# Second tiles of a pair turned through three PSUM banks, and w_down differences tied in order to products

## The chip, the cores and the metric

The kernel runs on one core of one Trainium2 chip. The metric is device time in microseconds (us) of one execution, as a median of three runs. A profile is one further execution, taken by the hardware profiler. PE is TensorE (matmuls and transposes), DVE is VectorE, ACT is ScalarE, POOL is GpSimd, SP is SyncE, whose queue issues most of the transfers.

## The reference

One decoder layer in float32 with S = 2048 tokens and D = 1024 channels. The feed-forward part, in which the change lies, has D_FF = 2816:

```python
hn = rms_norm(h, mix_pre_g)
proj = hn @ w_in                      # q, k, v and the convolution's input
attn_out = sliding_window_attention(q, k, v, attn_sinks, rel_bias)
conv_out = conformer_conv(u, ...)     # GLU, causal depthwise conv width 31, LayerNorm, swish, pointwise
mixed = jnp.concatenate([attn_out, conv_out], axis=-1) @ w_out
h = h + rms_norm(mixed, mix_post_g)
hn = rms_norm(h, ffn_pre_g)
ff = (jax.nn.silu(hn @ w_gate) * (hn @ w_up)) @ w_down
h = h + rms_norm(ff, ffn_post_g)
```

## The kernel before, in words

**Tiles and stages.** The tokens are cut into four tiles of 512 (tile 0 to 3). A tile passes through stages named by a letter that every buffer's name carries behind the @: A (input projection), B (attention), C (convolution taps, which DVE multiplies and adds into `fc` buffers), W (output projection, residual, norms), H (the normed tile turned so that channels lie on partitions, and operands made of it), F (gate and up products) and G (products with w_down, and the output). The work of several stages is emitted interleaved, by costs written beside each `yield`; a tile scheduler then fixes the order of each engine's instructions before the run. On the chip each engine works through its own order strictly and waits where a semaphore is not yet up.

**Products.** A float32 product is made of three matmuls on rounded parts: for each operand ACT copies the high part (`split_f`, L821) and DVE subtracts it from the operand to get the low part (`lo`, L825, recorded at L94 like nearly every DVE operation). A product of stage F is 12 matmuls of 128x512 into one of four `mm` banks of PSUM (L85). There are three banks called `tr` and one called `ct`; `tr` is used by the attention and by part of W, `ct` by the turns of H.

**Pairs of tiles.** Tiles 0 and 1, and tiles 2 and 3, are multiplied together with w_gate and w_up by a Strassen-Winograd scheme: seven products of half-size blocks in place of eight. Its token operands are called B11 and B21 (of the first tile of a pair), B22 (of the second) and T1 to T4 (sums over both). While the second tile is in stage W, stage F already runs the products that need the first tile only (`stage_pre`): a first half with B11, whose results go to DRAM (`keeps`), and a second half with B21, which is *seeded*: SP loads a kept result into a `gb` buffer (L923), ACT copies it into the PSUM bank (L939), and the 12 matmuls add to it. After that `stage_p1` runs the remaining products, which need T1 to T4 and B22.

**The turns and the sums.** At the end of stage W, `norm_w` holds the normed tile in four `chl` buffers. For the second tile of a pair (w = 1 and 3) it calls `turn_row` eight times. Each call takes a bank, does four 128x128 transposes on PE (L816), and has ACT copy the bank into a `mid` buffer, scaled by g_ffn (L817). The `chl` buffers come free with the last turn. `stage_h_sums` then makes the operands of the pair in four blocks of 256 channels: SP loads the first tile's turned rows from DRAM (`hT`, L868) into a `chl` buffer, DVE forms the sums (`chl@H`), and each sum is split by ACT and DVE into a high and a low part (`hl@H`, `ql@H`, `mid@H`, `p@H`, `yt@H`, `mb@H`).

**The differences of w_down.** The products with w_down use a like scheme, and its weight differences are made once, in `stage_tsums`, which runs beside the products of stage F of the first pair. For each of 11 pairs of row blocks POOL issues four loads of w_down (L1106) into a `wx` buffer (a ring of one) and two `fc` buffers (a ring of three, shared with the convolution taps), DVE subtracts four times (L1111, recorded at L94, `wx@G` and `fc@G`), and POOL issues four stores to DRAM (`td`, L1112).

**Ties.** `mat` (L77) records every matmul of a product in `made["rows"]`. The DVE wrapper (L86) already gives the convolution taps an order-only dependency on such a matmul: the scheduler has to place the tap behind it, but nothing waits on the chip.

Of the kernel before, what the change touches and what calls it, by code (L numbers as in the profile page):

```python
# [18 lines left out]
ALU = mybir.AluOpType  # L19
# [18 lines left out]
def layer_kernel(ctx, tc, x, xT, cols, rows, sinks, relb, onehot, w_in, w_pw, w_out, w_gate, w_up, w_down, out):  # L38
# [19 lines left out]
    def f4(tag, shape=(P, D)):  # L58
        return t_(tag, shape)

    def f2(tag, shape=(P, T)):
        return t_(tag, shape)
# [8 lines left out]
    def bank(tag, bufs):  # L71
        return ps.tile([P, T], F32, tag=tag, name=nm(tag), bufs=bufs)

    mm = lambda: bank("mm", 4)
    tr = lambda: bank("tr", 3)
    ct = lambda: bank("ct", 1)
# [4 lines left out]
    pace = {"main": None, "tied": None}  # L81
    made = {"rows": [], "at": 0, "new": True}
# [9 lines left out]
    def dve(op):  # L92
        def emit(*args, **kw):
            r = op(*args, **kw)  # L94
            if not paced[0]:
                pace["main"] = r.ins
            elif pace["main"] is not None and pace["main"] is not pace["tied"]:
                tc.add_manual_dep(
                    r.ins,
                    pace["main"].name,  # L100
                    mybir.DependencyInfo(mybir.DependencyClass.NoSync, mybir.DependencyReason.DATA),
                    reason="conv taps keep pace with the projections",
                )
                pace["tied"] = pace["main"]
            if paced[0] and made["rows"]:
                made["new"] = True
                tc.add_manual_dep(
                    r.ins,
                    made["rows"][min(made["at"], len(made["rows"]) - 1)].name,
                    mybir.DependencyInfo(mybir.DependencyClass.NoSync, mybir.DependencyReason.DATA),  # L110
                    reason="conv taps keep pace with the products",
                )
                made["at"] += TIE
            return r

        return emit

    stt = dve(nc.vector.scalar_tensor_tensor)
    vtt = dve(nc.vector.tensor_tensor)
# [639 lines left out]
    def norm_w(w, acc):  # L759
# [35 lines left out]
        if w == 0:  # L795
            normed.extend(xs)
        elif w == 2:
            for k in range(KC):
                u = turn_row(w, xs, k, f2("gb"))
                nc.scalar.dma_start(hT[1][k], u)  # L800
                yield 2.0
        else:
            for k in range(4):
                t = t_("mid", (P, 2, T))
                for j in range(2):
                    turn_row(w, xs, k + 4 * j, t[:, j])
                    yield 2.0
                normed.append(t)
# [2 lines left out]

    def turn_row(w, xs, k, u):
        lab[0] = f"H{w}"
        b = ct()
        for s in range(4):
            nc.tensor.transpose(b[:, s * P : (s + 1) * P], xs[s][:, k * P : (k + 1) * P], ident)  # L816
        act(u, b, AF.Copy, scale=g_ffn[:, k : k + 1])  # L817
        return u
# [27 lines left out]
    def stage_h_plain(ws, ops, n, off):  # L846
        L = f"H{ws[0]}"
        for k in range(4):
            lab[0] = L
            if ws[0]:  # L850
                u = f2(COLTAG[ws[0]][k])
                nc.sync.dma_start(u, hT[ws[0] // 2][k + off])
            else:
                u = turn_row(0, normed, k + off, f2("gb"))
                lab[0] = L
                nc.scalar.dma_start(hT[0][k + off], u)
            o = op_tile(ws, ops, n, k, {})
            act(o[:, 0], u, AF.Copy)
            lo(u, o, False)
            yield 2.0  # L860
# [238 lines left out]
    def stage_tsums(td):  # L1099
        L = "G0"  # L1100
        for pr in range(NF // 2):
            lab[0] = L
            wx = f4("wx", (P, 2, T))
            b = [wx[:, 0], wx[:, 1], f2("fc"), f2("fc")]
            for i, (f, n) in enumerate(((0, 0), (0, 1), (1, 0), (1, 1))):
                nc.gpsimd.dma_start(b[i], w_down[2 * pr + f, :, n * T : (n + 1) * T])  # L1106
            yield 3.9
            b11, b12, b21, b22 = b
            for to, o, p_, q_ in ((0, b11, b12, b11), (2, b12, b22, b12), (1, b22, b22, b11), (3, b21, b21, b22)):
                lab[0] = L  # L1110
                vtt(o, p_, q_, ALU.subtract)  # L1111
                nc.gpsimd.dma_start(td[to, pr], o)  # L1112
                yield 0.25

# [326 lines left out]
    lh.add("S0", stage_h_sums(ws, ops), lambda: "N1" in lh.done)  # L1441
    run(stage_pre(ws, ops, mids[0], keeps[0], Q0))
    lt.add("TS", stage_tsums(td))
    run(stage_p1(ws, ops, mids[0], keeps[0]))
    lt.until("TS")
# [80 lines left out]
```

## Time and profile before

| what | value |
|---|---|
| time, median of 3 runs | 1982.09 us (1979.29 to 1984.77) |
| the profiled execution | 1987.9 us, of which its span is 1986.2 us |
| PE busy | 1930.4 us, 97% of the span |
| PEld (weight loads, beside PE) | 1546.7 us, 78% |
| DVE busy | 1476.3 us, 74% |
| ACT busy | 961.8 us, 48% |
| POOL busy | 304.3 us, 15% |
| granted TensorE clock, mean | 0.987 of full speed |
| transfers | 435.67 MB, mean 219 GB/s |

The span is the time from the first to the last recorded instruction; 1.7 us of the profiled execution lie outside it. Busy shares are means over the whole span. The rows of a window show, for each engine, its busy us and the count of its instructions, then the granted clock as a share of full speed, the mean busy share of the 16 DMA engines, and what they moved in GB/s. Rows of a timeline show start, duration, engine, line, operation, output and inputs; what stands in square brackets is the idle time of the engine before it and what ended it.

### The profile page before, as it was taken

What the parts mean: (1) busy time and instruction counts of PE and PEld (TensorE: products, weight loads), DVE (VectorE), ACT (ScalarE), POOL (GpSimd) and SP (SyncE); (2) the same over time, 40 slices, a digit from 0 to 9 for tenths busy, and PEclk for the clock granted to TensorE, in tenths of its full rate; (3) what the DMA queues carried; (4) which work ended last, traced back from release to release, by engine and by line L of the source; (5) the groups of instructions that cost most, each with busy time, mean ns of one, the idle gap of its engine ahead of it and who ended that gap; (6) DMA issues with size and microseconds to landing.
All of it is one profiled execution on the core that took longest, in us unless ns stands there. A gap on an engine that the chain in (4) does not pass through costs nothing.

```text
span 1986.2 us, 26652 instructions
## 1 busy us (share of the span) xinstructions
PE 1930.4 (97%) x8730; PEld 1546.7 (78%) x8730; DVE 1476.3 (74%) x2648; ACT 961.8 (48%) x1886; POOL 304.3 (15%) x427
## 2 busy tenths in 40 slices
PE   8999999999999699999999999999899999999997
PEld 6877777777777588778888878887688888888886
DVE  5999969995874899787759965666866775555557
ACT  5455354447647544334345464656533433345443
POOL 4011011111121101220000110000023332311003
PEclk9999999999999799999999999999899999999999
DMA  8787657566658668775478777759844542375664
GB/s 311 251 303 219 210 187 256 185 212 214 225 195 281 232 218 266 260 266 184 130 253 276 259 255 242 249 202 309 293 140 169 179 140 96 132 244 181 211 195 144
DMA packets 209578, 435.67 MB, mean 219 GB/s; under 512 B 21752, under 2 KB 39328, under 8 KB 209440
## 3 DMA queue, kind: packets, MB, share of 16 engines
q1 hardware_dynamic: 191648, 402.52, 60.7%
q0 software_dynamic: 7040, 23.07, 3.5%
q10 hardware_dynamic: 10752, 8.39, 1.3%
q8 instruction: 68, 1.11, 0.2%
q14 instruction: 70, 0.57, 0.1%
HBM read 323.26 MB, written 110.63 MB: 218 GB/s over the span
## 4 chain that ended last, share of the span: by engine, by line
PE 77%; DVE 8%; DMA 7%; issue 3%; POOL 2%; ACT 2%; SPq 0%; DVEq 0%; POOLq 0%; ACTq 0%
PE mm@F L85 32%; PE mm@G L85 16%; PE mm@A L85 15%; PE mm@W L85 4%; PE tr@B L85 4%; PE tr@W L85 2%; DVE fc@C L94 2%; DMA wx@G<-w_down 1%; DMA gb@F<-keeps 1%; PE mm@U L85 1%; DVE w@F L94 1%; DVE hl@G L94 1%; PE tr@B L491 1%; DMA td<-wx@G 1%; DMA fc@G<-w_down 1%
## 5 line engine op out<-in xcount | busy, mean ns | idle before, releaser
L94 DVE SCALAR_TENSOR_TENSOR fc@C<-glu@C,colt,fc@C 128x512 f32<-128x512 f32 x480 | 357.3, 758 | 2.6
L85 PE MATMUL mm@F<-hl@H,w@F 128*128 128x512 f32 x1056 | 261.3, 397 | 10.2 <-ACT mm@F L939 10.2
L85 PEld LDWEIGHTS mm@F<-hl@H,w@F 128*128 128x128 f32 x1056 | 201.0, 192 | 54.6 <-ACT mm@F L939 12.5
L85 PE MATMUL mm@G<-hl@G,hl@G 128*128 128x512 f32 x924 | 227.7, 393 | 1.1 <-DVE hl@G L94 1.1
L821 ACT ACTIVATE w@F<-chl@F 128x512 fp32r<-128x512 f32 x220 | 135.9, 626 | 187.8 <-PE mm@F L85 149.6
L85 PE MATMUL mm@A<-hl@A,w@A 128*128 128x512 f32 x840 | 209.5, 397 | 4.2 <-ACT w@A L127 1.5
L85 PEld LDWEIGHTS mm@G<-hl@G,hl@G 128*128 128x128 f32 x924 | 171.7, 188 | 37.3 <-DVE hl@G L94 1.9
L85 PE MATMUL mm@G<-w@G,hl@G 128*128 128x512 f32 x876 | 199.4, 389 | 0.0
L85 PEld LDWEIGHTS mm@G<-w@G,hl@G 128*128 128x128 f32 x876 | 164.4, 188 | 34.1
L85 PEld LDWEIGHTS mm@A<-hl@A,w@A 128*128 128x128 f32 x840 | 156.6, 189 | 42.9 <-issue 3.3
L94 DVE TENSOR_TENSOR w@F<-chl@F,w@F 128x512 fp32r<-128x512 f32 x198 | 151.4, 768 | 49.0 <-ACT w@F L821 48.8
L85 PE MATMUL mm@F<-mid@H,w@F 128*128 128x512 f32 x528 | 136.5, 398 | 20.3 <-ACT w@F L821 13.3
L85 PEld LDWEIGHTS mm@F<-mid@H,w@F 128*128 128x128 f32 x528 | 101.0, 192 | 43.7 <-ACT w@F L821 14.1
L85 PE MATMUL mm@F<-ql@H,w@F 128*128 128x512 f32 x528 | 130.0, 392 | 0.0
L85 PE MATMUL mm@F<-p@H,w@F 128*128 128x512 f32 x528 | 129.1, 389 | 0.0
L85 PE MATMUL mm@F<-x@H,w@F 128*128 128x512 f32 x528 | 126.9, 391 | 0.0
L85 PEld LDWEIGHTS mm@F<-ql@H,w@F 128*128 128x128 f32 x528 | 99.1, 189 | 20.8
L85 PEld LDWEIGHTS mm@F<-p@H,w@F 128*128 128x128 f32 x528 | 99.1, 188 | 20.6
L85 PEld LDWEIGHTS mm@F<-x@H,w@F 128*128 128x128 f32 x528 | 98.4, 188 | 21.1 <-issue 0.8
L127 ACT ACTIVATE w@A<-raw@A 128x512 fp32r<-128x512 f32 x110 | 67.5, 626 | 92.1 <-PE mm@A L85 62.1
L94 DVE TENSOR_TENSOR w@G<-raw@G,w@G 128x512 fp32r<-128x512 f32 x73 | 52.1, 713 | 73.0 <-ACT w@G L821 71.8
L494 POOL TENSOR_SCALAR_AFFINE_SELECT p@B<-p@B 128x512 f32<-128x512 f32 x62 | 51.7, 843 | 338.4 <-ACT p@B L492 337.1
(314 smaller groups left out, 3290.1 us busy)
## 6 DMA issues: line engine op xcount, KB each, us to landing
mids<-fa@F SPq DMA_DIRECT2D x154, 256.0 KB, 2.7
raw@A<-w_in SPq DMA_DIRECT2D x55, 512.0 KB, 4.6
w@A<-lo_in SPq DMA_DIRECT2D x84, 256.0 KB, 3.3
fc@G<-mids SPq DMA_DIRECT2D x77, 256.0 KB, 3.4
fa@G<-mids SPq DMA_DIRECT2D x75, 256.0 KB, 4.4
gb@F<-keeps SPq DMA_DIRECT2D x72, 256.0 KB, 3.5
w@W<-fold SPq DMA_DIRECT2D x32, 512.0 KB, 5.9
raw@F<-w_gate SPq DMA_DIRECT2D x22, 512.0 KB, 4.0
```

The lines of the kernel that those rows point to most:

```text
L85: r = nc.tensor.matmul(*args, **kw)
L94: r = op(*args, **kw)
L127: act(w[:, 0], raw, AF.Copy)
L491: nc.tensor.transpose(o[:, i * P : (i + 1) * P], pr[:, 4 * g + i], ident)
L494: nc.gpsimd.affine_select(out=pg[:, kb].rearrange("p (i q) -> p i q", q=P), in_=pg[:, 1].rearrange("p (i q) -> p i q", q=P), compare_op=AL ...
L821: act(w[:, 0], x, AF.Copy)
```

## The change

`turn_row` takes its bank from the ring of three `tr` banks where w is odd, so for tiles 1 and 3; tiles 0 and 2 keep the one `ct` bank. In `stage_tsums` each of the 44 subtractions gets an order-only dependency on the product matmul that was emitted last. No instruction is added or taken away.

```diff
     def turn_row(w, xs, k, u):
         lab[0] = f"H{w}"
-        b = ct()
+        b = tr() if w % 2 else ct()
         for s in range(4):
             nc.tensor.transpose(b[:, s * P : (s + 1) * P], xs[s][:, k * P : (k + 1) * P], ident)
...
                 lab[0] = L
-                vtt(o, p_, q_, ALU.subtract)
+                r = vtt(o, p_, q_, ALU.subtract)
+                tc.add_manual_dep(
+                    r.ins,
+                    made["rows"][-1].name,
+                    mybir.DependencyInfo(mybir.DependencyClass.NoSync, mybir.DependencyReason.DATA),
+                    reason="weight differences keep pace with the products",
+                )
                 nc.gpsimd.dma_start(td[to, pr], o)
```

The change moves instructions, since the scheduler orders them anew. Each name below carries the number of its buffer, which is the same in both programs.

PE, before, among the seeded products of the first pair: one turn of tile 1, between matmuls of one product (`mm@F_1010`; `chl@W_938` to `941` are the four normed row blocks).

```order
L85 MATMUL mm@F_1010_6103<-hl@H_802_4927,w@F_994_6037 128x512 x3
L85 MATMUL mm@F_1010_6103<-hl@H_810_4970,w@F_994_6037 128x512 x3
L85 MATMUL mm@F_1010_6103<-hl@H_813_4981,w@F_994_6037 128x512 x3
L816 MATMUL ct@H_972_5927<-ident,chl@W_938_5731 128x128
L816 MATMUL ct@H_972_5927<-ident,chl@W_939_5733 128x128
L816 MATMUL ct@H_972_5927<-ident,chl@W_940_5735 128x128
L816 MATMUL ct@H_972_5927<-ident,chl@W_941_5737 128x128
L85 MATMUL mm@F_1010_6103<-hl@H_821_5028,w@F_994_6037 128x512 x3
```

PE, after, at the last product with B11 and the first seeded one (`mm@F_997`, `mm@F_996`): three turns begin together.

```order
L85 MATMUL mm@F_997_6044<-x@H_787_4853,w@F_975_5940 128x512 x3
L816 MATMUL tr@H_968_5902<-ident,chl@W_938_5731 128x128
L816 MATMUL tr@H_972_5927<-ident,chl@W_938_5731 128x128
L816 MATMUL tr@H_974_5934<-ident,chl@W_938_5731 128x128
L85 MATMUL mm@F_997_6044<-x@H_799_4916,w@F_975_5940 128x512 x3
L85 MATMUL mm@F_996_6042<-hl@H_802_4927,w@F_982_5975 128x512 x3
L85 MATMUL mm@F_996_6042<-hl@H_810_4970,w@F_982_5975 128x512
L816 MATMUL tr@H_968_5902<-ident,chl@W_939_5733 128x128
L816 MATMUL tr@H_968_5902<-ident,chl@W_940_5735 128x128
L816 MATMUL tr@H_972_5927<-ident,chl@W_939_5733 128x128
L816 MATMUL tr@H_974_5934<-ident,chl@W_939_5733 128x128
```

The eight turns of tile 1 stood one to every second product, with the last in product F_1081. They now stand in groups of three, three and two, with the last in F_1022, ten products earlier.

DVE, before, just ahead of `w@F_1104`, the first weight split that `stage_p1` needs for T1. The last split of a seeded product, `w@F_1092`, stands 52 rows ahead of it.

```order
L94 TENSOR_TENSOR chl@H_1059_6351<-chl@H_1059_6351,chl@H_1066_6379 128x512
L94 TENSOR_TENSOR wx@G_1119_6658<-fc@G_1121_6660,wx@G_1119_6658 128x512
L94 TENSOR_TENSOR ql@H_1071_6409<-chl@H_1066_6379,ql@H_1071_6409 128x512
L94 SCALAR_TENSOR_TENSOR fc@C_1083_6465<-glu@C_1082_6463,colt,fc@C_1083_6465 128x512
L94 TENSOR_TENSOR p@H_1077_6436<-chl@H_1059_6351,p@H_1077_6436 128x512
L94 TENSOR_TENSOR chl@F_1103_6599<-raw@F_1100_6592,chl@F_1101_6594 128x512
L94 TENSOR_TENSOR chl@F_1102_6596<-chl@F_1102_6596,raw@F_1100_6592 128x512
L94 TENSOR_TENSOR w@F_1104_6602<-chl@F_1102_6596,w@F_1104_6602 128x512
```

DVE, after, at the same split:

```order
L94 TENSOR_TENSOR p@H_1077_6436<-chl@H_1059_6351,p@H_1077_6436 128x512
L94 TENSOR_TENSOR w@F_1089_6494<-raw@F_1085_6471,w@F_1089_6494 128x512
L94 TENSOR_TENSOR fa@F_1076_6434<-fa@F_1076_6434,mm@F_1075_6420 128x512
L94 TENSOR_SCALAR fc@C_1083_6465<-glu@C_1082_6463,colt 128x512
L94 TENSOR_TENSOR w@F_1092_6517<-raw@F_1085_6471,w@F_1092_6517 128x512
L94 TENSOR_TENSOR mid@H_1078_6439<-chl@H_1059_6351,mid@H_1078_6439 128x512
L94 TENSOR_TENSOR chl@F_1102_6596<-chl@F_1102_6596,raw@F_1100_6592 128x512
L94 TENSOR_TENSOR chl@F_1103_6599<-raw@F_1100_6592,chl@F_1101_6594 128x512
L94 TENSOR_TENSOR w@F_1104_6602<-chl@F_1102_6596,w@F_1104_6602 128x512
```

The sums of stage H and their splits now stand among the weight splits of the seeded products, and four rows lie between `w@F_1092` and `w@F_1104`. The first difference of w_down (`wx@G_1116`) moved from row 751, among the rows of stages A to C, to row 1093; pairs of differences stood some 18 rows apart and now stand some 27 apart (15 to 46).

SP, after, in the seeded half of the first pair: the loads of `hT` for the sums (`chl@H`) among the loads of kept results (`gb@F`) and of weights (`raw@F`).

```order
L923 DMA gb@F_1039_6247<-keeps_4718 128x512
L868 DMA chl@H_1019_6152<-hT_115 128x2x512
L971 DMA mids_4715<-fa@F_1017_6147 128x512
L916 DMA raw@F_1049_6300<-w_gate 128x512
L923 DMA gb@F_1043_6268<-keeps_4718 128x512
L916 DMA raw@F_1049_6300<-w_up 128x512
L868 DMA chl@H_1036_6239<-hT_115 128x2x512
L923 DMA gb@F_1050_6303<-keeps_4718 128x512
L971 DMA mids_4715<-fa@F_1029_6205 128x512
L868 DMA chl@H_1059_6351<-hT_115 128x2x512
```

Before, these three loads stood 25 rows later, at rows 410, 414 and 418 for now 385, 390 and 393, and were the neighbours of `gb@F_1093` to `gb@F_1142`. In the second pair the four loads moved from rows 865 to 881 up to rows 832 to 866, and four loads of `chl@G` from `h_scr` now stand ahead of them, at rows 823 to 826.

## The prediction

> **What bounds the kernel now.** I read the page first: what is busy, and where the clock drops.
>
> ```profile
> span 1986.2 us, 26652 instructions
> PE 1930.4 (97%) x8730; PEld 1546.7 (78%) x8730; DVE 1476.3 (74%) x2648; ACT 961.8 (48%) x1886; POOL 304.3 (15%) x427
> PEclk9999999999999799999999999999899999999999
> ```
>
> PE sets the time; a gain can come only from the 56 us in which it is not busy and from slow clock. Two slices are below 9 inside the run (slices of 49.7 us: the 14th starts at 646 us, the 29th at 1390 us). PE's waits over the whole run, as total, times and longest:
>
> ```profile
> PE mm@F L85 <- ACT w@F L821: 13.3, 2, 12.6
> PE mm@F L85 <- ACT mm@F L939: 10.2, 6, 3.3
> PE mm@F L85 <- DVE w@F L94: 5.8, 2, 3.0
> PE mm@F L85 <- DVE at@F L94: 4.8, 2, 3.3
> ```
>
> All four are in stage F: the start of `stage_p1` (w@F), the seeds (L939), and DVE's accumulation (at@F). The windows of the first place, against a stretch without a wait (DVE is the third pair of numbers; then clock, DMA share, GB/s):
>
> ```profile
> 620.00:650.00 30.00, 30.00 (x143) 24.83 (x142) 12.90 (x20) 20.04 (x37) 0.00 (x0) 1.00 0.76 244
> 680.00:690.00 10.00, 1.91 (x4) 1.09 (x5) 10.00 (x18) 4.11 (x7) 0.89 (x2) 0.50 0.54 196
> 690.00:700.00 10.00, 10.00 (x35) 7.99 (x34) 10.00 (x17) 4.01 (x7) 2.72 (x6) 0.75 0.84 286
> 650.00:700.00 50.00, 34.39 (x140) 27.34 (x140) 46.12 (x76) 25.16 (x43) 7.56 (x15) 0.80 0.72 244
> 750.00:800.00 50.00, 50.00 (x222) 41.42 (x221) 45.32 (x74) 19.60 (x35) 10.23 (x19) 1.00 0.80 272
> ```
>
> Undisturbed, PE does 222 matmuls in 50 us, 0.2252 us each. In 650 to 700 it does 140: 82 are missing, 82 x 0.2252 = 18.5 us. DVE is 12.90 us busy in the 30 of 620 to 650 and full in 680 to 700. PE's timeline shows the turns of tile 1, then the stall:
>
> ```profile
> 645.05 0.60 PE L816 MATMUL ct@H<-ident,chl@W 128*128 128x128 f32 x4
> ...
> 656.44 0.60 PE L816 MATMUL ct@H<-ident,chl@W 128*128 128x128 f32 x4
> 656.80 15.69 PE L85 MATMUL mm@F<-hl@H,w@F 128*128 128x512 f32 x68
> 685.10 1.22 PE L85 MATMUL mm@F<-mid@H,w@F 128*128 128x512 f32 x2 [12.61 <-ACT w@F L821]
> 689.31 2.08 PE L85 MATMUL mm@F<-mid@H,w@F 128*128 128x512 f32 x4 [3.00 <-DVE w@F L94]
> ```
>
> The wait names ACT, but the split it waited for is fed by DVE. DVE's timeline over the stall, from the first sum of stage H to the split that released PE, with differences of w_down in between:
>
> ```profile
> 657.39 0.68 DVE L94 TENSOR_TENSOR chl@H<-mid@W,chl@H 128x512 f32<-128x512 f32 x1
> ...
> 665.40 0.69 DVE L94 TENSOR_TENSOR wx@G<-fc@G,wx@G 128x512 f32<-128x512 f32 x1
> ...
> 688.57 0.69 DVE L94 TENSOR_TENSOR w@F<-chl@F,w@F 128x512 fp32r<-128x512 f32 x1
> ```
>
> The sums begin 1 us after the last turn; then DVE is 31.2 us without a gap before the weight split of `stage_p1` comes, 51 rows at 0.61 us. PE has only the 15.7 us of products already split. So the turns, 5.7 us apart (three from 645.05 to 656.44) because one bank serves them, hold the sums, and the sums hold the splits.
>
> **First pair: the ring.** In the new order the last turn is in F_1022 instead of F_1081, ten products earlier; a product is 12 matmuls, 2.70 us, so the sums may start 27 us sooner and lie among the seeded products, where DVE idles 17.1 us in 30, 0.57. In those 27 us and the 15.7 that PE has in hand, 24 us are idle. Of the 31.2 us, five w_down differences (3 us, by the tie) and eight convolution taps (5 us) now stand behind w@F_1104; the 23 us left just fit. Ahead of that split stand 4 rows, 2.4 us, where there were 52. Bounds are 9 us, if the splits of the sums still crowd out half of it, and 18.5; DVE never falls behind PE by more than the three products split ahead when I count its new rows, so I take 18.5. The turns on PE stay 32 transposes a tile; three at once occupy it for 3 x 0.60 = 1.8 us, as much in sum as before.
>
> The Trainium skill ("TensorE: Matmul & The Clock Gate", Part 1) says that the array falls to half clock after about 3.4 us idle and needs about as long busy to return; the row 680 to 690 with 0.50 agrees, and by that rule a cured wait of 15.6 us returns some 1.7 to 3 us more than its length. Counting missing matmuls includes this already (18.5 for 12.61 + 3.00).
>
> What the ring costs: SP's three `hT` loads (512 KB each) move 25 rows up, past `gb` loads, into the seeded products. Their neighbourhood gets about 2 MB more with the first loads of `stage_p1`. The transfers there, and in the second pair's seeded part where the DMA engines are full (first row 620 to 672 us, second 1340 to 1440 us; KB each, us to landing):
>
> ```profile
> gb@F<-keeps SPq DMA_DIRECT2D x18, 256.0 KB, 3.1
> ...
> gb@F<-keeps SPq DMA_DIRECT2D x18, 256.0 KB, 5.2
> ```
>
> A seed is needed every 2.70 us and its load is asked for two products ahead (5.4 us), so 3.1 us is hidden and 5.2 us just fails. The lower bound is 0 to 1 us (hidden), the upper 11.0 us (as in the second pair, worked out below). DMA share is 0.76 now, and 2 MB more over 25 us add 80 GB/s to 244: some 324, between this and the 350 of the second pair below. A load that lands in between, at 4 to 5 us, mostly meets its 5.4. I take 3 us.
>
> **First pair: the tie.** Each difference now follows the product matmul emitted last; it gives no wait on chip, so bounds are the positions. DVE's waits in 690 to 900 us, a wait of DVE and two of PE there, the window, and POOL's transfers (median us to landing) from 700 to 900:
>
> ```profile
> DVE wx@G L94 <- DMA wx@G<-w_down: 9.1, 3, 6.5
> DVE wx@G L94 <- DMA fc@G<-w_down: 7.1, 4, 3.8
> 809.18 0.69 DVE L94 TENSOR_TENSOR wx@G<-wx@G 128x512 f32<-128x512 f32 x1 [6.51 <-DMA wx@G<-w_down]
> 813.18 1.67 PE L85 MATMUL mm@F<-mid@H,w@F 128*128 128x512 f32 x6 [1.19 <-DVE fa@F L94]
> 821.78 2.93 PE L85 MATMUL mm@F<-yt@H,w@F 128*128 128x512 f32 x6 [3.28 <-DVE at@F L94]
> 800.00:900.00 100.00, 94.01 (x406) 76.71 (x406) 83.06 (x135) 36.37 (x64) 22.06 (x41) 0.98 0.80 268
> td<-wx@G POOLq DMA_DIRECT2D x18, 256.0 KB, 4.0
> wx@G<-w_down POOLq DMA_DIRECT2D x16, 256.0 KB, 5.2
> ```
>
> DVE stands for 16.2 us on w_down loads whose buffers the previous pair had just left; behind it on DVE lie fa@F and at@F, for which PE waits. In 800 to 900 PE does 406 matmuls of 444; 38 are missing, 8.6 us. The new order puts pairs 27 rows apart (16 us at 0.61) instead of 18 (11 us), against a store and a load of 4.0 + 5.2 = 9.2 us, so most loads land in time; two gaps of 15 rows (9 us) remain. Bounds 0 and 8.6 us; I take 8.6 - 1.6 = 7.0 us, 1.6 being one wait of the size of the smaller ones, 7.1 us in 4. The `wx` and `fc` buffers are held longer and convolution taps share the `fc` ring; I cost that at nothing, covered by DVE's slack once the waits are gone. The last pair now stands beside F_1408, well ahead of the last products F_1486 of the stage, so `td` is stored long before stage G reads it. POOL issues the same loads and stores; it is 15% busy.
>
> **Second pair: the ring.** Windows of its seeded part, and PE's waits from 1340 to 1440 us:
>
> ```profile
> 1370.00:1420.00 50.00, 41.90 (x173) 32.91 (x172) 35.18 (x70) 28.88 (x54) 0.00 (x0) 0.93 1.00 350
> 1420.00:1440.00 20.00, 16.53 (x60) 12.76 (x59) 18.74 (x30) 10.65 (x20) 4.71 (x1) 0.83 0.62 211
> PE mm@F L85 <- ACT mm@F L939: 8.1, 5, 3.3
> PE mm@F L85 <- DVE w@F L94: 2.8, 1, 2.8
> ```
>
> First row: 173 matmuls of 222, 49 missing, 11.0 us, at a DMA share of 1.00: seeds late. Second: 60 of 89, 29 missing, 6.5 us, where DVE is full (18.74 of 20) of sums before the first split, as in the first pair. The ring cures the latter; SP's `hT` loads, and four `chl@G` loads ahead of them, come earlier into a stretch where the DMA engines are full, so the former may grow. Bounds: +12 (the 6.5 and half of the 11.0, since bytes that leave the first row lie earlier, before the seeds) and -6 (nothing of the 6.5 cured, and five waits grown by 1.2 us each). I take +5: the 6.5 less 1.5.
>
> Sum: 18.5 - 3 + 7 + 5 = 27.5 us. The profiled execution's 1987.9 us (span 1986.2) becomes 1960.4; it lies 5.8 above the median 1982.1, so against that it is 1954.6, called **1955**. A difference of 0.3%, 6 us, is the least that I call one.
>
> **The rivals.** *Seeds late in the first pair too* (B): the moved loads fill the DMA engines there. For: three 512 KB loads plus the first of `stage_p1` go past `gb` loads; against: the share is 0.76, and the second pair also carries stores of outputs. It costs 11.0 instead of 3, and nothing is gained in the second pair: 18.5 - 11.0 + 7 = 14.5, 1967.6. The Trainium skill ("Trainium Kernel Development and Optimization", Key Constraints) speaks for it: transfers of SP, ACT and POOL run on the same 16 engines and interleave; 3.1 against 5.2 us agrees.
>
> *The order does not do what it says* (C): differences still wait for their loads, since one `wx` buffer must be emptied, stored and loaded in turn, and the second pair, bound by seeds, gives nothing: 18.5 - 3 = 15.5, 1966.6. For: 9.2 us of landings, and POOL issues eight of them in turn; against: 16 us between pairs. B and C together give 7.5: 1974.6.
>
> *Slower* (D): SP stands at an `hT` load of the second pair until its `chl` buffer, held by residual rows (`chl@G`) until the outputs are stored, is free; `gb` loads queue behind it and PE waits on every seed. In the new order the loads `chl@H_2090` and `2108` stand right behind `out` stores. Landings from 1340 to 1440 us:
>
> ```profile
> chl@H<-hT SPq DMA_DIRECT2D x4, 512.0 KB, 5.5
> out<-x@G SPq DMA_DIRECT2D x8, 256.0 KB, 3.3
> ```
>
> Each of four loads would hold the queue for 3.3 us and DVE's sums for 5.5 more, 8.8 x 4 = 35 us, and as DVE runs strictly in order the weight splits stand behind the sums: with the 5 us gain gone, 1955 + 5 + 35 = 1995. It decides when more than 28 of the 35 us show; at half, 17 us, the result is 1977, no change. Against: each load stands some rows before its first sum, and PE itself is late there by seeds, which gives DVE time.
>
> **How the numbers follow.** Forecast 0.61 (1955; its own range 1944 to 1965 by the bounds), B 0.14, C 0.10, both 0.02, D at half 0.05, D in full 0.08. Faster by over 0.3%: 0.61 + 0.14 + 0.10 + 0.02 = 0.87; within: 0.05; slower: 0.08. Low end: 18.5 - 1 + 8.6 + 12 = 38.1, 1944. High end: B and C, with 4 us for the difference of medians (half of the spread 1979.29 to 1984.77, and more), 1972; beyond lie both together and D, 0.15, and little below.
>
> **What would show it.** In the changed profile, PE's 12.6 us wait for w@F is gone and 650 to 700 us holds about 215 matmuls or more at a clock near 1.00; DVE is busier in 620 to 650 than 12.9 of 30. Waits on L939 in the first pair stay under 4 us in sum (B: near 8, and `gb` lands in 5 us). DVE's waits on w_down fall from 16.2 to under 5 us (C: stay above 10). The second pair keeps most of its L939 waits and loses the last two stalls (D: they grow past 30, with SP in the wait). I would be wrong if PE waited for w@F at the start of `stage_p1` as long as before, for then the bank was not what held the sums.

## The result, and the profile after

The changed kernel takes 1970.43 us (median of 6 runs, 1967.51 to 1974.62) beside 1985.26 us for the kernel before (6 runs, 1979.29 to 1989.89). The ratio is 0.9932, 95% interval 0.9914 to 0.995, which is 13.5 us faster (9.9 to 17.1). The forecast was 27.5 us, to 1955: the sign is right, the size is twice what was measured. The profiled execution took 1974.62 us with a span of 1972.5; a second one of the same kernel, made with the experiments, 1968.1 with a span of 1966.0.

The windows of the first pair in the changed kernel, which answer to those shown of before (PE busy and count, PEld, DVE, ACT, POOL, clock, DMA share, GB/s):

```profile
620.00:650.00 30.00, 28.68 (x137) 23.51 (x136) 21.78 (x36) 25.55 (x46) 0.00 (x0) 1.00 0.78 262
650.00:700.00 50.00, 48.57 (x211) 38.99 (x210) 45.57 (x75) 26.43 (x49) 5.92 (x11) 1.00 0.81 271
700.00:900.00 200.00, 194.61 (x851) 158.55 (x849) 175.94 (x285) 76.63 (x134) 35.30 (x66) 1.00 0.73 247
```

And the last row of the kernel before:

```profile
700.00:900.00 200.00, 194.01 (x848) 159.52 (x847) 176.68 (x286) 77.75 (x135) 37.11 (x69) 0.99 0.76 251
```

The stall at the start of `stage_p1` is gone: 211 matmuls in 650 to 700 for 140 before, 71 x 0.2252 = 16.0 us. DVE does in 620 to 650 what it did later: 21.78 us busy for 12.90. But from 700 to 900 the count is 851 for 848, against some 888 undisturbed (222 in 50 us): the loss that the tie was to take away is still there.

PE's timeline at the turns of tile 1 and at the first product of `stage_p1` (`ql@H` and `mid@H` mark it):

```profile
622.45 1.47 PE L816 MATMUL tr@H<-ident,chl@W 128*128 128x128 f32 x12
628.36 1.03 PE L816 MATMUL tr@H<-ident,chl@W 128*128 128x128 f32 x8
...
672.70 3.01 PE L85 MATMUL mm@F<-hl@H,w@F 128*128 128x512 f32 x12 [0.68 <-ACT mm@F L939]
675.63 1.42 PE L85 MATMUL mm@F<-ql@H,w@F 128*128 128x512 f32 x5
676.90 1.53 PE L85 MATMUL mm@F<-mid@H,w@F 128*128 128x512 f32 x6
```

The last turn ends before 630 us, not at 657, and the step from seeded products to `stage_p1` has no wait for w@F. Where the time still goes shows in the waits, first of DVE from 690 to 900 us, then of PE over the whole run:

```profile
DVE wx@G L94 <- DMA fc@G<-w_down: 9.7, 4, 3.4
DVE wx@G L94 <- DMA wx@G<-w_down: 0.8, 1, 0.8
```

```profile
PE mm@F L85 <- ACT mm@F L939: 15.1, 6, 5.2
PE mm@F L85 <- DVE at@F L94: 5.3, 5, 2.6
```

DVE's waits on w_down fell from 16.2 to 10.5 us only, and PE's waits for at@F did not fall (4.8 before). The waits for seeds (L939) grew from 10.2 to 15.1 us. Of these, 12.6 lie in the second pair, at 1350 to 1400:

```profile
1350.00:1400.00 50.00, 37.39 (x140) 29.41 (x140) 44.75 (x94) 31.21 (x62) 0.00 (x0) 0.86 0.98 344
1400.00:1440.00 40.00, 40.00 (x178) 33.14 (x177) 23.37 (x33) 18.81 (x34) 2.63 (x2) 1.00 0.63 214
```

The two late stalls there are cured (no wait for w@F after 1400), and 82 matmuls are now missing in 1350 to 1400 while the DMA engines are full (0.98). The loss moved from the start of `stage_p1` to the seeds.

### The profile page after: what moved, and what is told of

It is laid out like the page before. It is cut to its first block, busy times and chain, and to the rows that moved or that the text cites. A ratio compares the mean times of both kernels' runs of the same rounds, so it can differ in the third digit from the quotient of the medians.

```text
span 1972.5 us, 26663 instructions
## 1 busy us (share of the span) xinstructions
PE 1928.2 (98%) x8730; PEld 1544.7 (78%) x8730; DVE 1474.9 (75%) x2648; ACT 959.2 (49%) x1886; POOL 299.3 (15%) x427
## 4 chain that ended last, share of the span: by engine, by line
PE 78%; DVE 8%; DMA 7%; issue 3%; ACT 3%; POOL 1%; SPq 0%; DVEq 0%; POOLq 0%; ACTq 0%
PE mm@F L85 31%; PE mm@G L85 18%; PE mm@A L85 15%; PE mm@W L85 5%; PE tr@B L85 4%; PE tr@W L85 3%; DVE fc@C L94 2%; PE mm@U L85 1%; DVE w@F L94 1%; DMA mids<-fa@F 1%; PE tr@B L491 1%; DVE chl@F L94 1%; DMA raw@F<-w_gate 1%; DVE fa@F L94 1%; DMA raw@A<-w_in 1%
## 5 line engine op out<-in xcount | busy, mean ns | idle before, releaser
L85 PE MATMUL mm@F<-hl@H,w@F 128*128 128x512 f32 x1056 | 259.3, 396 | 15.3 <-ACT mm@F L939 15.1
L85 PE MATMUL mm@F<-mid@H,w@F 128*128 128x512 f32 x528 | 131.6, 389 | 0.0
```

Source lines behind the costliest of these rows:

```text
L85: r = nc.tensor.matmul(*args, **kw)
```

## The experiments

All times are medians, and each ratio is to the kernel before, run beside it.

**The parts alone.** The ring without the tie:

```diff
-                r = vtt(o, p_, q_, ALU.subtract)
-                tc.add_manual_dep(r.ins, made["rows"][-1].name, ...)
+                vtt(o, p_, q_, ALU.subtract)
```

> The ring for tiles 1 and 3, without the tie on the w_down differences. Theory (the ring on tile 1 is the whole gain, since it moves the sums of stage H ahead of the first split of stage_p1): 10 to 16 us faster than before, ratio 0.992 to 0.995, PE's 12.6 us wait for w@F gone, DVE's waits on w_down loads 8 to 16 us as in both kernels. Rival (the tie is what clears DVE for the sums): under 6 us faster, and a wait for w@F of 4 us or more left at the start of stage_p1.

Measured: 1970.58 us, ratio 0.994 (0.9923 to 0.9957): as fast as the change itself within the intervals. PE's long wait for w@F is gone, and DVE waits 13.5 us on w_down in 700 to 900, as the theory had it. The tie without the ring:

```diff
-        b = tr() if w % 2 else ct()
+        b = ct()
```

> The tie on the w_down differences, with the one ct bank for all turns. Theory: 0 to 4 us faster than before, ratio 0.998 to 1.000; of the 12.6 us wait for w@F at most the 3 us of five differences go, DVE's waits on w_down stay above 8 us, since a load is only issued when the store behind the difference before it has left the buffer, wherever DVE does that difference. Rival (the tie gives the 7 us forecast): 6 to 10 us faster, DVE's waits on w_down under 5 us.

Measured: 1982.53 us, ratio 0.9997 (0.9985 to 1.0008), no difference. Its profile still has the stall before `stage_p1`:

```profile
682.16 1.22 PE L85 MATMUL mm@F<-mid@H,w@F 128*128 128x512 f32 x2 [9.60 <-ACT w@F L821]
685.83 1.22 PE L85 MATMUL mm@F<-ql@H,w@F 128*128 128x512 f32 x2 [2.45 <-ACT w@F L821]
```

These waits are 12.1 us for 15.6 (12.61 and 3.00): about 3 us did leave the stretch, as forecast, but the time does not show them. The theory missed on w_down: DVE waits there for 6.5 us, not over 8. The ring for tile 1 alone, with the tie:

```diff
-        b = tr() if w % 2 else ct()
+        b = tr() if w == 1 else ct()
```

> The tie, and the ring for tile 1 only; tile 3 keeps the ct bank. Theory (the second pair's seeded part is bound by its transfers, so faster turns there only change which wait is shown): within 3 us of the changed kernel, ratio to before 0.992 to 0.995. Rival (the second pair earned the forecast 5 us and it was lost elsewhere): 4 to 7 us slower than the changed kernel, ratio 0.996 or more.

Measured: 1970.93 us, ratio 0.9933 (0.9918 to 0.9949), the same as with both tiles. So the ring on tile 1 carries the gain, and the ring on tile 3, as the kernel stands, gives nothing that these intervals show. PE's waits in the second pair (1290 to 1460 us), with the one bank on tile 3 and then with the ring on both (the changed kernel), show why the theory was right that faster turns there change little but which wait is shown:

```profile
PE mm@F L85 <- ACT mm@F L939: 8.8, 6, 3.2
PE mm@F L85 <- ACT w@F L821: 2.8, 1, 2.8
```

```profile
PE mm@F L85 <- ACT mm@F L939: 12.6, 3, 5.2
```

**What DVE's waits on w_down cost.** First, the differences moved to POOL (`ptt` is `nc.gpsimd.tensor_tensor`):

```diff
-                r = vtt(o, p_, q_, ALU.subtract)
+                r = ptt(o, p_, q_, ALU.subtract)
```

> The changed kernel with the 44 w_down differences made by POOL instead of DVE, so that no DVE instruction waits for a w_down load. Theory (DVE's waits on those loads are what PE's waits for at@F in the first pair come from): PE's 5.3 us of waits for at@F fall under 2 us, 3 to 8 us faster than the changed kernel, ratio to before 0.989 to 0.992. Rival (those PE waits come from DVE's own work and from the loads of mids): the at@F waits stay at 4 us or more, within 2 us of the changed kernel, ratio 0.992 to 0.994; or slower, if POOL, which also issues the loads and stores, falls behind.

Measured: 2002.55 us, ratio 1.0093 (1.0077 to 1.0108), 32 us slower than the change. The rival had allowed for slower, by a POOL that falls behind, but not for this much. DVE no longer waits for w_down at all, but PE's waits for at@F are 18.0 us, and the same DVE operations became longer. Groups of DVE in 700 to 900 us (count, busy us, mean ns), with POOL's differences, then in the changed kernel:

```profile
L94 DVE TENSOR_TENSOR w@F<-chl@F,w@F 128x512 fp32r<-128x512 f32 x66 | 53.0, 806 | 9.1 <-ACT w@F L821 9.1
L94 DVE SCALAR_TENSOR_TENSOR fc@C<-glu@C,colt,fc@C 128x512 f32<-128x512 f32 x43 | 36.0, 837 | 0.1
```

```profile
L94 DVE TENSOR_TENSOR w@F<-chl@F,w@F 128x512 fp32r<-128x512 f32 x71 | 48.2, 682 | 1.3 <-ACT w@F L821 1.3
L94 DVE SCALAR_TENSOR_TENSOR fc@C<-glu@C,colt,fc@C 128x512 f32<-128x512 f32 x43 | 31.8, 741 | 0.0
```

This run does not answer the question, because it brought in a cost of its own. The next one leaves the work out:

```diff
         for pr in range(NF // 2):
-            wx = f4("wx", (P, 2, T))
-            b = [wx[:, 0], wx[:, 1], f2("fc"), f2("fc")]
...
+            if pr == 0:
+                wx = f4("wx", (P, 2, T))
...
+                if pr == 0:
+                    r = vtt(o, p_, q_, ALU.subtract)
...
+                    for k in range(NF // 2):
+                        nc.gpsimd.dma_start(td[to, k], o)
```

> The changed kernel with the loads and differences of only the first of the 11 pairs of w_down row blocks; all 44 stores are made from those four results, so 40 loads and 40 differences are left out. Theory (DVE's waits on w_down loads, which the tie did not remove, are what PE's waits for at@F in the first pair come from): those PE waits fall from 5.3 us to under 2, and the time is 4 to 9 us under the changed kernel, ratio to before 0.989 to 0.991. Rival (they come from the loads of mids and from how full DVE is): the waits for at@F stay at 4 us or more, within 2 us of the changed kernel.

Measured: 1961.49 us, ratio 0.9892 (0.9876 to 0.9908), 8 to 9 us under the change in its first measurement and 5 to 8 in its second (0.9918, below), and 1.1 us of waits for at@F. The price put on those waits (7.0 of 8.6 us) was about right, though this kernel also leaves out 40 subtractions, some 27 us of DVE's work. The tie did not remove the waits.

**Why it did not.** POOL's timeline in the changed kernel, from the end of one pair to the next pair's second difference, which needs the load that is issued last, and then DVE's:

```profile
733.92 0.54 POOL L1118 DMA_DIRECT2D td<-fc@G  x1 [1.19 <-DVE fc@G L94]
738.63 0.54 POOL L1106 DMA_DIRECT2D fc@G<-w_down  x1 [4.17 <-DMA td<-fc@G]
741.11 0.54 POOL L1118 DMA_DIRECT2D td<-wx@G  x1 [1.95 <-DVE wx@G L94]
750.41 0.54 POOL L1106 DMA_DIRECT2D fc@G<-w_down  x1 [8.75 <-DVE chl@F L94]
```

```profile
732.95 0.68 DVE L94 TENSOR_TENSOR fc@G<-fc@G,fc@G 128x512 f32<-128x512 f32 x1
740.14 0.67 DVE L94 TENSOR_TENSOR wx@G<-wx@G 128x512 f32<-128x512 f32 x1
756.82 0.69 DVE L94 TENSOR_TENSOR wx@G<-fc@G,wx@G 128x512 f32<-128x512 f32 x1 [3.00 <-DMA fc@G<-w_down]
```

The `wx` loads of a pair go out once the pair before has left `wx`, here at 731.65. The two `fc` loads come later: the first at 738.63, when the last difference (732.95) has been made and stored, the other at 750.41, which also waits for a buffer of the `fc` ring that a convolution channel holds. (Most likely it waits for the channel's store, which SP issued at 746.24 and which took 3.6 us; the releaser in brackets is only the DVE row that ended at that time.) For the load that is needed second, what counts is the time from the last difference of a pair to the second of the next. The forecast used the time from first to first. If this is so, more distance between pairs must cure it. The lane that emits the differences (a lane advances its stage at a rate `RT` against the others) was slowed, and the operand of the second difference loaded first:

```diff
-    RT = 0.2
+    RT = 0.16
...
-            b = [wx[:, 0], wx[:, 1], f2("fc"), f2("fc")]
-            for i, (f, n) in enumerate(((0, 0), (0, 1), (1, 0), (1, 1))):
+            b22 = f2("fc")
+            b = [wx[:, 0], wx[:, 1], f2("fc"), b22]
+            for i, f, n in ((0, 0, 0), (1, 0, 1), (3, 1, 1), (2, 1, 0)):
```

> The changed kernel with two edits on the w_down differences: the lane that emits them runs at 0.16 in place of 0.2, so that pairs stand further apart, and b22, which the second difference needs, is allocated and loaded before b21. The whole result is computed. Theory (a load is issued as soon as the pair before has left its buffer, so only distance between pairs gives it time): DVE's waits on w_down fall from 10.5 to under 4 us, PE's waits for at@F in the first pair from 5.3 to under 3, and the time is 3 to 8 us under the changed kernel, ratio to before 0.989 to 0.992. Rival (the fourth load waits for the convolution channel that shares the ring, wherever the pairs stand): waits of 8 us or more stay, within 2 us of the changed kernel.

Measured: 1959.74 us, ratio 0.9866 (0.9845 to 0.9888), 9 us under the change run beside it (1969.0), a little more than the theory's 3 to 8. DVE's waits on the differences' loads of w_down are gone, and its windows are nearly full:

```profile
650.00:700.00 50.00, 49.14 (x214) 39.30 (x213) 46.52 (x76) 24.73 (x46) 4.97 (x10) 1.00 0.76 268
700.00:900.00 200.00, 200.00 (x884) 165.69 (x883) 178.07 (x287) 79.78 (x140) 29.50 (x55) 1.00 0.72 243
```

884 matmuls for 851 are 33 x 0.2252 = 7.4 us. Which of the two edits does it, and whether the tie has a part in it, two more kernels tell: the slower lane alone (`RT = 0.16`, loads in the old order), and both edits without the tie.

> The changed kernel with the slower lane alone; b21 is still loaded before b22. Theory (distance between pairs is what gives the loads time): within 3 us of the kernel with both edits, ratio to before 0.986 to 0.988, waits on w_down under 4 us. Rival (the load that comes last is the one that is needed first): waits of 6 us or more, ratio 0.990 or more.

Measured: 1959.54 us, ratio 0.9876 (0.9862 to 0.9889), no waits of the differences on w_down. The slower lane alone does it, with the tie in place.

> The ring, the slower lane and b22 first, without the tie. Theory (the scheduler needs the tie to keep a difference from moving ahead of its time; without it the pairs stand 15 to 20 rows apart whatever the lane says): DVE's waits on w_down of 6 us or more, and 4 to 10 us slower than the kernel with the tie, ratio to before 0.990 to 0.994. Rival (the lane alone spaces the loads): within 3 us of the kernel with the tie, ratio 0.986 to 0.988.

Measured: 1966.52 us, ratio 0.9908 (0.9894 to 0.9921), 7.0 us of waits on w_down. The loss lies elsewhere than expected, though. Windows of this kernel, and of the ring-only kernel:

```profile
650.00:700.00 50.00, 45.50 (x193) 35.36 (x192) 44.65 (x74) 23.72 (x44) 7.56 (x14) 1.00 0.82 287
700.00:900.00 200.00, 199.62 (x881) 164.98 (x880) 178.08 (x288) 79.09 (x138) 30.66 (x57) 1.00 0.70 239
```

```profile
650.00:700.00 50.00, 45.02 (x194) 35.62 (x193) 44.80 (x74) 23.78 (x44) 7.00 (x13) 1.00 0.81 276
700.00:900.00 200.00, 191.77 (x836) 155.93 (x835) 172.90 (x282) 75.87 (x133) 37.68 (x70) 1.00 0.75 253
```

Without the tie 650 to 700 holds 193 or 194 matmuls. With it the spaced kernel holds 214 and the changed kernel 211, in its second profile 205: 2 to 5 us. Without the tie the second difference of the first pair is made at 670 or 671 us, ahead of the first product of `stage_p1` (676); with it the first is made at 677 to 679, behind that product. PE waits there for seeds 3 to 4 us without the tie and about 1 us with it; that the early differences make these seeds late was not tested. The lane, more than the tie, fills 700 to 900 (881 without the tie, 884 with it; at the old rate 836 and 851). By the times the tie is worth 6 to 8 us beside the slower lane (0.9908 against 0.9876 and 0.9866), close to the 7 of the forecast, but mostly in another place. At the old rate it is worth 2 to 4 us (0.994 against 0.9932 and 0.9918), which the intervals of 0.002 on either side do not separate from nothing.

One rival stays open. The slower lane does two things: it gives the loads time, and it takes work off DVE in the crowded stretch, since 26 differences fall in 700 to 900 where the changed kernel has 32, some 4 us less. The kernel without the tie speaks for a part of the second: it keeps 7.0 us of DVE's waits on w_down there, none over 2.3 us, and yet PE waits for at@F only 0.4 us. So DVE's waits are not in themselves what PE loses; probably they cost PE time only where DVE has no slack left.

**The second pair.** The 16 seeds of `stage_pre` left out, so that the B11 part is not added there, with the ring on tile 3 and then without it (the condition stands in `fetch` and in `seed`):

```diff
-            if PRE <= q < q1:
+            if PRE <= q < q1 and not ws[0]:
...
-            product(o, wops.pop(q), ops[bn], not half)
+            fresh = not half or bool(ws[0])
+            o = mm() if fresh else seeded.pop(q)
+            product(o, wops.pop(q), ops[bn], fresh)
```

> The changed kernel without seeds in the second pair's stage_pre: the 16 gb loads and their copies are left out and the B21 products start from zero, so the B11 part is not added there. Theory (PE waits for seeds, because the DMA engines are full): PE's 12.6 us of waits on L939 in the second pair vanish and nothing of size takes their place, 10 to 18 us under the changed kernel, ratio to before 0.984 to 0.988. Rival (DVE and the weight loads are as late): waits for w@F of 5 us or more appear there, under 6 us gained.

> The same without the second pair's seeds, and with the turns of tile 3 in the one ct bank. Theory (the ring on tile 3 would be worth the forecast 5 us, and only the late seeds hide it): 3 to 8 us slower than its neighbour with the ring, with a wait for w@F of 3 us or more at the start of the second pair's stage_p1. Rival (the ring on tile 3 is worth nothing in either case): within 2 us of it.

Measured: 1951.53 us, ratio 0.9839 (0.9822 to 0.9855), with the ring, and PE has no wait at all in 1290 to 1460; 1965.48 us, 0.9908 (0.9893 to 0.9924), with the one bank. There PE waits again for the sums:

```profile
1402.23 1.22 PE L85 MATMUL mm@F<-mid@H,w@F 128*128 128x512 f32 x2 [9.05 <-ACT w@F L821]
1405.24 1.22 PE L85 MATMUL mm@F<-hl@H,w@F 128*128 128x512 f32 x2 [1.79 <-ACT w@F L821]
```

So the ring on tile 3 is worth 14 us where there are no seeds, more than the theory's 3 to 8, and the seeds take some 16 to 18 us in the changed kernel (0.9918 and 0.9932 against 0.9839). The four kernels together show the overlap. With the one bank PE waits 10.8 us for the sums where there are no seeds, and only 2.8 where it also waits 8.8 for seeds: DVE makes most of the sums in that time. With the ring the 2.8 are gone and the waits for seeds are 12.6, so nothing is left to gain. Why the seeds come late is not settled by this: the DMA engines are full (0.98 in 1350 to 1400), but SP, which issues the loads, also stood 6.6 us there for DVE's `fa@F`.

What would help the seeds? Fewer products ahead of `stage_p1`, then more (`PRES = {0: 20, 2: 12}` and `{0: 20, 2: 20}` for 16), and outputs emitted earlier (the lane's rate for O0.1 to E0.3 at 1.0 for 0.6):

> The changed kernel with 12 products with B11 and 12 seeded ones in the second pair, not 16 each; the whole result is still computed. Theory (too many bytes in too short a time): four seeds less, so the waits on L939 there fall from 12.6 to under 9 us, 1 to 6 us under the changed kernel. Rival (the products ahead of stage_p1 are the cover for the sums of stage H): waits for w@F of 5 us or more at the start of stage_p1, and slower than the changed kernel.

> The changed kernel with 20 products with B11 and 20 seeded ones in the second pair, not 16 each; the whole result is computed. Theory (the seeded part moves a fixed surplus of outputs, residual rows and hT loads, and more products only spread it over more time): the waits on L939 there fall from 12.6 to 6 to 10 us and the time is 1 to 5 us under the changed kernel. Rival (each seeded product brings its own bytes, so more of them wait alike): the waits stay at 12 us or more, and the time is the same or up to 4 us over.

> The changed kernel with the lane that emits the outputs of the first pair (O0.1, O0.3, E0.1, E0.3) at 1.0 in place of 0.6, so that outputs and residual rows are moved earlier, ahead of the second pair's seeds. The whole result is computed. Theory (what makes the seeds late is other traffic beside them): waits on L939 there under 9 us, 2 to 6 us under the changed kernel. Rival (the residual loads wait for buffers that only the last turn of tile 3 frees, so the traffic cannot come earlier): waits stay at 11 us or more, within 2 us.

Measured: 12 products 1975.88 us, ratio 0.9964 (0.9949 to 0.9979): slower than the change. The waits on L939 stay at 11.0 us and 6.2 us of waits for w@F come on top, so the cover is what was lost, as the rival said. 20 products: 1961.74 us, 0.9878 (0.9859 to 0.9897), L939 at 7.5 us for 12.6: about 7 us under the change, somewhat more than expected. Outputs earlier: 1968.6 us, 0.9915 (0.9898 to 0.9933), L939 at 10.7, between theory and rival: no difference in time from the change. Beside these two ran the changed kernel itself:

> The changed kernel itself once more, for a second profile and more times. Both theories: ratio to before 0.991 to 0.995; PE's waits of the first pair within 2 us and of the second within 4 us of the first profile, which is then the spread that one profile has.

Measured: 1969.0 us, ratio 0.9918 (0.9903 to 0.9934); waits for at@F 4.3 us (5.3 in the first profile), for seeds of the second pair 12.3 (12.6). The span differs by 6.5 us between the two profiles, most of it outside these waits.

**A version that beats both.** Spaced differences and 20 products in the second pair, and the same with 22:

> Spaced w_down differences (lane at 0.16, b22 first) and 20 products of each half in the second pair, in one kernel that computes the whole result. Theory (the two losses lie in different pairs and add): about 11 + 8 us under the changed kernel, ratio to before 0.980 to 0.985. Rival (what one gives the other takes): 0.986 or more.

> The same with 22 products of each half in the second pair, so that all gate and up blocks start ahead of stage_p1. The whole result is computed. Theory (a fixed surplus of traffic spread over more time): waits on L939 in the second pair no longer than with 20, ratio within 0.002 of its neighbour's or lower. Rival (each further seed brings bytes of its own, and keeps cost a store and two loads each): slower than its neighbour by 2 to 6 us.

Measured: 1952.61 us, ratio 0.984 (0.9827 to 0.9854), and 1954.08 us, 0.9848 (0.9832 to 0.9864). By the first ratio it is 31.7 us under the kernel before (29.0 to 34.3). Spaced alone is 26.6 and 20 products alone 24.2, and both contain the change's own 13.5 to 16.3 (its two measurements), so adding them would give 34 to 37: the gains add nearly in full. 22 products are neither better nor worse than 20.

## Why the forecast came out twice too large

The measured gain is 14 us short of the forecast. Two steps failed, the tie's 7 us and the second pair's 5; the ring on tile 1 was sized some 2 to 3 us too large.

**The ring on tile 1, 18.5 us less 3 for its seeds.** Right in mechanism, somewhat too large. In the profile 16.0 us return in 650 to 700, and 6 matmuls fewer in 620 to 650 take 1.4 back. By the times, the ring on tile 1 is the difference between 0.9997 (tie alone) and 0.9933 (tie and this ring), 12.7 us. The 18.5 was every matmul missing in 650 to 700, and 11 of the 82 are still missing there. The 3 us for late seeds in the first pair were not needed: `gb` lands in 3.8 us there for 3.1, and PE's waits on L939 in the first pair are 2.5 us for 2.1. The rival of seeds late in the first pair (B) did not happen.

```profile
gb@F<-keeps SPq DMA_DIRECT2D x17, 256.0 KB, 3.8
```

**The tie, 7 us.** This step failed, and with it rival C came true in its first half: the differences still wait for their loads. The price was about right (5 to 9 us when the work is left out, 7.4 in the windows of the spaced kernel; the 1.6 taken off for one smaller wait should be 1.8, 7.1 in 4); that the tie removes it was wrong: alone it gave a ratio of 0.9997, and with it 700 to 900 holds 851 matmuls for 848. The prediction set 16 us from pair to pair against 9.2 us of landings. But the load that the second difference needs starts only after the last difference of the pair before and its store, and at times after a convolution channel too. The sharing of the `fc` ring, which the prediction put at nothing, seems to cause one of the three waits of 700 to 900 (3.0 of 8.5 us). A tie that moves the differences moves these loads along.

**The second pair, +5 us.** This step failed too. Of its bounds, +12 to -6, nothing measurable came out (0.9933 with tile 1 alone, 0.9932 with both). The prediction cured one wait (6.5 us) and priced the other one (11.0 us of late seeds) as if they stood one behind the other. They overlap: while PE waits for seeds DVE makes the sums, so the wait that was left for the ring to cure was 2.8 us (10.8 where there are no seeds). The ring cured it, and the waits for seeds grew by at least as much (8.8 to 12.6 us, one profile each), where 1.5 us had been allowed. That the moved `hT` loads did this is not shown. In matmuls, 1350 to 1440 us lacks 73 with the one bank on tile 3, 82 with the ring and 72 in the ring's second profile: the late stretch was filled, and the same loss came back earlier. This is rival C's second half. C as a whole, given a chance of 0.10, is what happened, and its 15.5 us under before is close to the measured 13.5.

**The slower rival (D).** Nothing of it: the waits for seeds grew to 12.6 us, not past 30, and SP stood at its `hT` loads there for 1.2 us in sum (0.9 for the landing of residual rows, 0.3 for an output).

**The starting point.** The profiled execution of before was 1987.9 us, against medians of 1983 to 1985 in the later runs of the same kernel. The terms were counted in an execution whose stalls were perhaps 3 to 5 us larger than usual; the runs do not separate this.

## What to carry to other kernels

An order-only tie moves an instruction, and the loads that wait for its buffer move along: before a tie is costed, follow the ring of buffers backwards from the load to the last use before it, and take the gap from that use, not from one first use to the next. Two waits in one stretch are not two terms of a sum: while an engine waits for the one, the work behind the other gets done, so curing the smaller may give nothing until the larger is gone. A gain that vanished can be found by taking the suspected bottleneck out entirely, once with the change and once without it.

## What the runs showed of the hardware that was not expected

With 44 subtractions of 128x512 on POOL, at 1.4 to 1.5 us each, some of DVE's operations beside them take longer: `w@F` 806 ns in the mean for 682, a convolution tap 837 for 741, and single ones 2.43 us:

```profile
774.32 2.43 DVE L94 TENSOR_TENSOR w@F<-chl@F,w@F 128x512 fp32r<-128x512 f32 x1
776.67 1.74 DVE L94 TENSOR_TENSOR chl@F<-chl@F,raw@F 128x512 f32<-128x512 f32 x1
```

The Trainium skill ("GPSIMD Engine Reference", Key points) says that GpSimd shares its SBUF interfaces with VectorE and contends with DVE instructions that have two SBUF inputs; these rows agree. An operation that has one input in SBUF and the other in PSUM (an `mm` bank) takes as long as before; with POOL's differences, then in the changed kernel, in 700 to 900 us:

```profile
L94 DVE TENSOR_TENSOR at@F<-at@F,mm@F 128x512 f32<-128x512 f32 x26 | 17.1, 681 | 10.3 <-PE mm@F L85 10.3
```

```profile
L94 DVE TENSOR_TENSOR at@F<-at@F,mm@F 128x512 f32<-128x512 f32 x30 | 19.9, 678 | 5.2 <-PE mm@F L85 5.2
```

How much of the 32 us comes from this is not shown: PE's waits for seeds in the first pair also rose, from 2.5 to 10.0 us, with the DMA engines at a share of 0.90 to 0.92 in 620 to 700 us, for 0.78 to 0.81.
